# Inverting 64-row triangular blocks in pieces of 16, with gate copies and a weight split moved, in a one-layer RWKV-7 and window-attention step

## The chip, the cores and the metric

One core of one Trainium2 chip runs the whole program. The metric is device microseconds of one execution. The five engines have their own instruction queues, each worked off in order: PE (TensorE, matrix products; its weight loads are shown as PEld), DVE (VectorE), ACT (ScalarE), POOL (GpSimd) and SP (SyncE, which here only issues DMA transfers). A wait at the head of a queue holds everything behind it.

## The reference, cut to what matters

A prompt of 1024 tokens and 64 sample tokens (8 sequences of 8) pass through one layer: RMSNorm, one wide input projection, then two branches. Branch A is attention over a window of 128 with sinks. Branch B is RWKV-7: for each of 16 heads a 64x64 state is carried over the tokens.

```
z = ps + (prev - ps) * mu                      # token shift of r, k, v and two low-rank inputs
decay, a = f(w0 + tanh(wl) @ w2), sigmoid(a0 + al @ a2)      # the low-rank weights w2, a2
S_t = S_{t-1} * w_t + (S_{t-1} a_t) b_t^T + v_t k_t^T ;  y_t = S_t r_t
yb = (groupnorm(y) + bonus) * silu(gb)         # gb: the gate columns of the projection
out = x + (sigmoid(ma) * (ya @ w_out_a) + sigmoid(mb) * (yb @ w_out_b)) @ w_o ; y = RMSNorm(out)
```

The state is advanced by chunks of 64 tokens. Inside a chunk, the tokens depend on each other through a strictly triangular 64x64 matrix A made of the products of the keys, and the chunk needs the inverse of (I - A): one per chunk and head.

## The kernel before, in words

Products with the large weights are split: each fp32 operand is a high and a low part, and three products (hi·hi, hi·lo, lo·hi) are added (`mm3`, L183). A tile of 128 weight columns is `dense` (L190): three chunks of 364, 364 and 360 tokens, 24 matmuls each, into PSUM tiles `d` of which there are two; after each chunk a function `evac` empties the tile. The weights of the next tile are loaded ahead (`load_w`, L163): a DMA of `wraw`, ACT makes `whi`, POOL makes `wlo` (L171).

The program has four parts. `start` (L282) norms x and runs the first three tiles of weights; PE, SP and POOL take its instructions in the order in which they are written. At its end, for each of 8 groups, SP loads the low-rank weights (`lr`), ACT and DVE split them, and SP writes both parts to DRAM (`d_c`, L384 to L390). `rwkv` (L493) is branch B together with most of the input projection. `attention` (L1005) and `final` (L1314) follow.

`rwkv` works in 16 steps s = 4p + q: a pair p of head groups (2 groups x 2 heads) and a quarter q of the prompt (256 tokens, 4 chunks; in q = 3 also the 64 sample tokens). Each step has generators:

- `front` (L569): `quarter` twice (elementwise work on r, k, decay), `arrays`, `scores` (the products `A`, L775, of which the triangular parts are kept in `ab`), then the inversion, then `bonus` and `turn`.
- `invert` (L812): 32 diagonal blocks of 32x32 (16 matrices, two blocks each; 40 blocks in q = 3) go through DRAM (`s1`) into a layout of three partitions per block, and DVE substitutes row after row: 31 rounds of two instructions, L832 (product `Tt`) and L834 (sum `TR`), on up to 96 elements per partition. The inverses go back through DRAM (`s2`).
- `merge` (L839): loads them into `ti` (L855), transposes (DVE, L856), and makes the off-diagonal 32x32 quarter of each 64x64 inverse with two rounds of 16 small matmuls (`q_..a`, `q_..b`) and a DVE copy between (L867).
- `chain` (L877): four chunks in a row; in each PE and DVE hand to each other three times: `c<-vsu,X`, DVE copy `xs` (L910), `c<-xs,ti`, DVE copy `vsu` (L915), `c<-vsu,kbt`, DVE update `vsu` (L926).
- `posts` and `samples`: group norm and output of a step; the sample tokens.

Beside them runs `stream`: the dense tiles of the projection. Its evacuations are `shift_tile` (L398: two scaled copies by ACT, sum by POOL, and one column carried from the last chunk by DVE, L411), `gate` (L438: ACT makes the sigmoid in three passes from PSUM, then DVE multiplies it with the PSUM tile, L444, and SP writes `d_g`) and `spill` (L449: the same for gates of branch A at L460). Tiles `zz` and `pad` of these evacuations have two buffers each.

Two things set the order. PE's is written out by `drive` (L142): it keeps a clock of its own, adds a price for each matmul (`mm`, L111) and takes next the generator whose due time comes first; a generator says how long it has to wait (`yield mark, time`). So `merge` is placed `WI` = 38 after the mark `f` of its front, and its first matmul `WM` = 5 later; dense matmuls fill the time between. The order on DVE, ACT, POOL and SP comes from a scheduler by priorities: chains and merges 400000, fronts, samples and posts 200000, dense 0; `INV` is 0 here, so the inversion stands where its front stands.

Of the kernel before, what the change touches and what calls it, by code (L numbers as in the profile page):

```python
# [25 lines left out]
NG = 8  # L26
# [3 lines left out]
FRONT, CHAIN, SAMP, POST, DENSE, INV = 200000, 400000, 200000, 200000, 0, 0  # L30
# [10 lines left out]
WI, WD, WB, WA, WM, WH, WS, WP, WT, WR, WE = 38.0, 3.5, 4.0, 2.0, 5.0, 1.4, 2.4, 5.0, 10.0, 3.0, 12.0  # L41
# [40 lines left out]
class Prog:  # L82
# [199 lines left out]
    def start(self, xp, w0):  # L282
# [115 lines left out]
    def shift_tile(self, idx, ti, out):  # L398
# [5 lines left out]
        def evac(c0, c1, ps):  # L404
# [44 lines left out]
    def spill(self, idx, dst, kind="copy", scale=1.0):  # L449
# [3 lines left out]
        def evac(c0, c1, ps):  # L453
# [3 lines left out]
            else:  # L457
                self.sig_neg(t, t, ps, -1.0, 0.0)
                if kind == "silu":
                    nc.vector.tensor_tensor(t, ps, t, ALU.mult)  # L460
# [32 lines left out]
    def rwkv(self):  # L493
# [28 lines left out]
        for t in (self.ti, self.tss):  # L522
            nc.gpsimd.memset(t, 0.0)
        for t in self.xs:
# [44 lines left out]
    def front(self, s):  # L569
# [22 lines left out]
        s1 = self.dp.tile([2, 2 * nh, 32, 32], F32, name=f"s1{nm}")  # L592
        for h in range(2):
            for i in range(2):
                r = 64 * h + 32 * i
                nc.sync.dma_start(s1[i, h * nh:h * nh + nh].rearrange("n j t -> j n t"), f["ab"][r:r + 32, :nh, 32 * i:32 * i + 32])
        f["s1"], n2 = s1, 2 * nh
        with self.tc.high_priority(offset=INV):
            self.invert(nm, n2, f)
# [35 lines left out]
    def prefetch(self, g, q):  # L635
# [7 lines left out]
        nc.sync.dma_start(w2.bitcast(F32).rearrange("p x j c -> p x (j c)"), self.d_c[:, g])  # L643
# [168 lines left out]
    def invert(self, nm, n2, f):  # L812
# [3 lines left out]
        ab, s1 = f["ab"], f["s1"]  # L816
        nb = 2 * n2
        s2 = self.dp.tile([nb, 33, 32], F32, name=f"s2{nm}")
        np_ = 3 * nb
        M = [ep.tile([P, 16, 32 - 16 * x], F32, tag=f"TM{x}", name=f"TM{x}{nm}", bufs=1) for x in range(2)]  # L820
        R = ep.tile([P, 11, 32], F32, tag="TR", name=f"TR{nm}", bufs=1)
        tmp = ep.tile([P, 128], F32, tag="Tt", name=f"Tt{nm}", bufs=1)
        for x in range(2):
            for k in range(3):
                nc.sync.dma_start(M[x][:np_].rearrange("(b k) j t -> k b j t", k=3)[k],
                                  s1.rearrange("i n j t -> (i n) j t")[:, 16 * x:16 * x + 16, 16 * x:])
        nc.sync.dma_start(R[:np_], self.I["ri"][:np_].rearrange("p (a b) -> p a b", a=11))
        for s in range(31):
            w = 31 - s
            cc = s // 3 + 1  # L830
            tv = tmp[:np_, :cc * w].rearrange("p (c t) -> p c t", c=cc)
            nc.vector.tensor_tensor(tv, M[s // 16][:np_, s % 16:s % 16 + 1, s + 1 - 16 * (s // 16):].to_broadcast([np_, cc, w]),  # L832
                                    R[:np_, 0:cc, s:s + 1].to_broadcast([np_, cc, w]), ALU.mult)
            nc.vector.tensor_tensor(R[:np_, 0:cc, s + 1:32], R[:np_, 0:cc, s + 1:32], tv, ALU.add)  # L834
        for k in range(3):
            nc.sync.dma_start(s2.rearrange("b (c k) t -> k b c t", k=3)[k], R[:np_].rearrange("(b k) c t -> k b c t", k=3)[k])
        f["s2"] = s2

    def merge(self, s):  # L839
        nc = self.nc  # L840
        nm = f"{s // 4}_{s % 4}"
        yield f"f{s}", WI
        if s:
# [3 lines left out]
        f = self.fr[s]  # L847
        ab, nh = f["ab"], f["nh"]
        sv = f["s2"][:, :32, :].rearrange("(i n) j t -> i j n t", i=2)
        tv = self.ti.rearrange("p i c x -> p (i c) x")  # L850
        for h in range(2):
            r = 64 * h
            for i in range(2):
                b = r + 32 * i
                nc.sync.dma_start(tv[b:b + 32, :, b:b + 32], sv[i][:, h * nh:h * nh + 8, :])  # L855
            nc.vector.transpose(ab[r:r + 32, 0:8, 0:32], tv[r:r + 32, :, r:r + 32])  # L856
            if nh == 10:
                for i in range(2):
# [697 lines left out]
```

## Time and profile before

| | us |
|---|---|
| median of 3 runs | 1932.51 (1928.37 to 1935.75) |
| the profiled execution | 1925.88 |
| its span, first to last instruction | 1924.1 |
| PE busy / DVE / ACT / POOL in the span | 1665.7 / 1239.1 / 911.9 / 510.8 |
| mean granted clock of PE, of full speed | 0.929 |

A matmul's row gives its own duration, and matmuls overlap; distances between starts tell the rate. "Idle before" is the time in which the engine did nothing before an instruction, and the name behind "<-" is what ended the wait. The granted clock is 1.0 at 2.4 GHz and 0.5 at 1.2 GHz; means lie between.

### The profile page before, as it was taken

Reading aid. Unit: us, or ns where it says so; the run is one execution under the profiler, and the core shown is the slowest. Engines: PE = TensorE matmul, PEld = TensorE weight load, DVE = VectorE, ACT = ScalarE, POOL = GpSimd, SP = SyncE. Lnnn points to the kernel's source line nnn. Section 1 sums busy time; section 2 is a strip of 40 time slices with the busy share of each in tenths; the row PEclk is TensorE's granted clock in tenths of the full one; section 3 lists DMA queues with packets and bytes.
Section 4 is the critical chain, followed back from the end, with each engine's and each line's share of the span. In section 5 each row is a group of like instructions: output and inputs, shape, how many; then the busy total and the mean of one; then the engine's idle time right before and its main releaser. Section 6 shows DMA issues by size and latency. Waiting matters only on the chain.

```text
span 1924.1 us, 33459 instructions
## 1 busy us (share of the span) xinstructions
PE 1665.7 (87%) x11744; PEld 1570.1 (82%) x11744; DVE 1239.1 (64%) x3667; ACT 911.9 (47%) x2270; POOL 510.8 (27%) x654
## 2 busy tenths in 40 slices
PE   6839978868878878886987888799999999999997
PEld 4739977768777878876877888799999999899997
DVE  6202468768768877867778777874266777644543
ACT  5314544435445545544545556553466665522232
POOL 4236424323424432442343323233300010000000
PEclk7869989878989988987988999899999999999999
DMA  4233433324333433333333344223622343374531
GB/s 164 89 121 115 122 96 96 104 74 112 99 97 114 113 104 100 110 82 96 111 99 103 106 116 117 83 79 99 198 79 72 92 148 118 114 243 141 174 108 58
DMA packets 236795, 214.98 MB, mean 112 GB/s; under 512 B 134996, under 2 KB 205252, under 8 KB 236596
## 3 DMA queue, kind: packets, MB, share of 16 engines
q1 hardware_dynamic: 221844, 162.70, 29.4%
q0 software_dynamic: 14784, 50.15, 7.9%
q8 instruction: 93, 1.52, 0.3%
q14 instruction: 74, 0.61, 0.1%
HBM read 147.58 MB, written 67.16 MB: 112 GB/s over the span
## 4 chain that ended last, share of the span: by engine, by line
PE 48%; DVE 27%; DMA 8%; issue 7%; ACT 4%; POOL 3%; SPq 2%; DVEq 0%; POOLq 0%; ACTq 0%
PE d L110 29%; DVE Tt L832 6%; DVE TR L834 5%; PE wo L110 5%; PE c L110 2%; DVE vsu L926 2%; PE s L110 2%; DVE KB L711 2%; PE A L110 2%; PE o L110 2%; DMA wraw<-in_w 2%; PE pt L108 1%; DMA TM<-s 1%; PE y L110 1%; DMA lr<-in_lora 1%
## 5 line engine op out<-in xcount | busy, mean ns | idle before, releaser
L110 PE MATMUL d<-hhi,whi 128*128 128x364 f32 (+1 forms) x1656 | 588.9, 356 | 127.1 <-DVE gz L444 46.8
L110 PE MATMUL d<-hlo,whi 128*128 128x364 f32 (+1 forms) x1656 | 569.6, 344 | 10.2 <-DVE hlo L352 8.7
L110 PEld LDWEIGHTS d<-hhi,whi 128*128 128x128 f32 x1656 | 331.5, 200 | 138.4 <-DVE gz L444 50.1
L110 PEld LDWEIGHTS d<-hlo,whi 128*128 128x128 f32 x1656 | 331.2, 200 | 18.3 <-DVE hlo L352 13.2
L110 PE MATMUL d<-hhi,wlo 128*128 128x364 f32 (+1 forms) x1656 | 339.4, 343 | 0.0
L110 PEld LDWEIGHTS d<-hhi,wlo 128*128 128x128 f32 x1656 | 287.5, 197 | 3.9 <-issue 2.9
L171 POOL TENSOR_TENSOR wlo<-wraw,whi 128x1024 fp32r<-128x1024 f32 x56 | 137.1, 2448 | 201.9 <-ACT whi L170 74.1
L832 DVE TENSOR_TENSOR Tt<-TM,TR 96x90 f32<-96x90 f32 (+26 forms) x496 | 157.1, 317 | 23.1 <-DMA TM<-s 10.2
L834 DVE TENSOR_TENSOR TR<-TR,Tt 96x90 f32<-96x90 f32 (+26 forms) x496 | 135.6, 273 | 12.7
L170 ACT ACTIVATE whi<-wraw 128x1024 fp32r<-128x1024 f32 x90 | 95.0, 1056 | 85.3 <-PE d L110 61.3
L902 POOL TENSOR_TENSOR sp<-vsu,pc 64x128 f32<-64x128 f32 x128 | 63.2, 494 | 236.8 <-DVE vsu L926 218.6
L414 POOL TENSOR_TENSOR zz<-zz,pad 128x364 f32<-128x364 f32 (+1 forms) x75 | 71.6, 955 | 105.2 <-ACT zz L413 70.0
L1390 POOL TENSOR_TENSOR xr<-xr,frs 128x256 f32<-128x256 f32 x2 | 1.8, 932 | 342.6 <-ACT frs L1387 342.6
L926 DVE SCALAR_TENSOR_TENSOR vsu<-c,pc,sp 64x64 f32<-64x64 f32 x240 | 67.9, 283 | 26.7 <-PE c L110 23.3
L412 ACT ACTIVATE pad<-d,prm 128x364 f32<-128x364 f32 (+1 forms) x75 | 40.8, 543 | 91.4 <-PE d L110 58.1
L1129 ACT ACTIVATE sc<-sc,st 128x256 f32<-128x256 f32 (+1 forms) x128 | 61.8, 485 | 28.4 <-DVE st L1125 28.2
L110 PE MATMUL d<-yhi,whi 128*128 128x364 f32 (+1 forms) x192 | 63.8, 333 | 0.0
L110 PE MATMUL d<-ylo,whi 128*128 128x364 f32 (+1 forms) x192 | 63.8, 332 | 0.0
L110 PE MATMUL d<-ol,whi 128*128 128x364 f32 (+1 forms) x192 | 63.1, 329 | 0.7 <-DVE ol L230 0.7
L110 PE MATMUL d<-oh,whi 128*128 128x364 f32 (+1 forms) x192 | 63.2, 329 | 0.0
L711 DVE TENSOR_TENSOR KB<-e,sg 64x256 f32<-64x256 f32 x128 | 61.8, 497 | 1.2
L110 PEld LDWEIGHTS c<-vsu,kbt 128*128 128x128 f32 x256 | 37.7, 202 | 30.0 <-DVE vsu L915 29.3
(329 smaller groups left out, 3617.9 us busy)
## 6 DMA issues: line engine op xcount, KB each, us to landing
wraw<-in_w POOLq DMA_DIRECT2D x56, 512.0 KB, 4.1
wraw<-in_w SPq DMA_DIRECT2D x37, 512.0 KB
d_z<-zz POOLq DMA_DIRECT2D x48, 182.0 KB, 2.2
w<-d_c SPq DMA_DIRECT2D x32, 256.0 KB
zv<-d_z SPq DMA_DIRECT2D x48, 128.0 KB
d_m<-sp SPq DMA_DIRECT2D x32, 182.0 KB
stageo<-d_o SPq DMA_DIRECT2D x8, 544.0 KB
d_z<-zz POOLq DMA_DIRECT2D x24, 180.0 KB, 4.1
```

Of the source, the lines that this page charges most:

```text
L108: self.nc.tensor.transpose(out, lhsT, rhs)
L110: self.nc.tensor.matmul(out, lhsT=lhsT, rhs=rhs, **kw)
L170: nc.scalar.activation(hi, raw, AF.Copy)
L171: (nc.vector if self.dve_lo else nc.gpsimd).tensor_tensor(lo, raw, hi.bitcast(F32), ALU.subtract)
L412: nc.scalar.activation(pad[:, 1:1 + m], ps[:, :m], AF.Copy, scale=mu)
L414: nc.gpsimd.tensor_tensor(z[:, :m], z[:, :m], pad[:, 0:m], ALU.add)
L711: nc.vector.tensor_tensor(KB[hr, :4, j, :], self.v64(t)[hr], self.d64(Pi, 1)[hr], ALU.mult)
L832: nc.vector.tensor_tensor(tv, M[s // 16][:np_, s % 16:s % 16 + 1, s + 1 - 16 * (s // 16):].to_broadcast([np_, cc, w]), R[:np_, 0:cc, s:s + ...
L834: nc.vector.tensor_tensor(R[:np_, 0:cc, s + 1:32], R[:np_, 0:cc, s + 1:32], tv, ALU.add)
L902: nc.gpsimd.tensor_tensor(sp[h], vsu[h, c, :, h], pc[h, c].unsqueeze(2).to_broadcast([64, 2, HD]), ALU.mult)
L926: nc.vector.scalar_tensor_tensor(dst, pn[h, i, h], pc[h, c, i:i + 1], sp[h, i], ALU.mult, ALU.add)
L1129: nc.scalar.activation(sc[k], sc[k], AF.Exp, bias=st[:, 0, k:k + 1], accum_out=st[:, 1, k:k + 1])
```

## The change: what it does

The diff has four parts. (1) The inversion substitutes in diagonal blocks of 16: two partitions per block, 15 rounds of two DVE instructions on at most 36 elements. In q = 3 the sample matrices are inverted by a second call. `merge` now puts the inverses into `dinv` with 8 loads (4 from SP, 4 from POOL), and builds 32x32 and then 64x64 inverses by four rounds of small matmuls (32, 32, 16 and 16) with DVE work between; only its last part waits for the chain of the step before. (2) The gates of branch B, and of branch A in `spill`, are copied from PSUM by ACT, and POOL multiplies; POOL writes `d_g`. (3) The low-rank weights are no longer split in `start`: in a group's first quarter `prefetch` loads the raw weights into a `zz` buffer, splits them on ACT and DVE into the tile that is used, and writes them to `d_c` for the other three quarters. (4) The column carried between chunks is copied by ACT. Beside that: `INV` is 150000, `WI` is 24, and the planner's price of a 32-row matmul is 0.024.

```diff
-FRONT, CHAIN, SAMP, POST, DENSE, INV = 200000, 400000, 200000, 200000, 0, 0
+FRONT, CHAIN, SAMP, POST, DENSE, INV = 200000, 400000, 200000, 200000, 0, 150000
...
-        self.clk += max(n / 2190, 0.085) if rhs.dtype == F32R else ...
+        self.clk += 0.024 if rhs.shape[0] == 32 else max(n / 2190, 0.085) if rhs.dtype == F32R else ...
...  start
-        for g in range(NG):
-            raw, hi, lo = (xp.tile([P, 364], F32, tag="sq", name=f"l{x}{g}", bufs=4)[:, :2 * P] for x in "rhl")
-            nc.sync.dma_start(raw, self.I["lora"][:, g].rearrange("p j c -> p (j c)"))
-            nc.scalar.activation(hi.bitcast(F32R), raw, AF.Copy)
-            nc.vector.tensor_tensor(lo.bitcast(F32R), raw, hi, ALU.subtract)
-            for x, t in enumerate((hi, lo)):
-                nc.sync.dma_start(self.d_c[:, g, x], t)
...  shift_tile
-                nc.vector.tensor_copy(pad[:, 0:1], prev[0][:, 364:365])
+                nc.scalar.activation(pad[:, 0:1], prev[0][:, 364:365], AF.Copy)
...  gate (spill: the same with `sx`, without the DMA)
-            self.sig_neg(t, t, ps, -1.0, 0.0)
-            nc.vector.tensor_tensor(t, ps, t, ALU.mult)
-            nc.sync.dma_start(self.d_g[g][:, c0:c1], t)
+            x = ep.tile([P, 369], F32, tag="pad", name=f"gx{g}_{c0}", bufs=2)[:, :c1 - c0]
+            nc.scalar.activation(x, ps, AF.Copy)
+            self.sig_neg(t, t, x, -1.0, 0.0)
+            nc.gpsimd.tensor_tensor(t, x, t, ALU.mult)
+            nc.gpsimd.dma_start(self.d_g[g][:, c0:c1], t)
...  prefetch
-        nc.sync.dma_start(w2.bitcast(F32).rearrange("p x j c -> p x (j c)"), self.d_c[:, g])
+        w2v = w2.bitcast(F32).rearrange("p x j c -> p x (j c)")
+        if q:
+            nc.sync.dma_start(w2v, self.d_c[:, g])
+        else:
+            raw = ep.tile([P, 364], F32, tag="zz", name=f"w2r{nm}", bufs=2)[:, :2 * P]
+            nc.sync.dma_start(raw, self.I["lora"][:, g].rearrange("p j c -> p (j c)"))
+            nc.scalar.activation(w2[:, 0].rearrange("p j c -> p (j c)"), raw, AF.Copy)
+            nc.vector.tensor_tensor(w2[:, 1].rearrange("p j c -> p (j c)"), raw, w2v[:, 0], ALU.subtract)
+            nc.sync.dma_start(self.d_c[:, g], w2v)
...  invert
+        for a in range(2):
+            for k in range(2):
+                nc.sync.dma_start(M[nb * a:nb * a + nb].rearrange("(b k) j t -> k b j t", k=2)[k], s1[:, 16 * a:16 * a + 16, 16 * a:16 * a + 16])
-        for s in range(31):
-            w = 31 - s
-            cc = s // 3 + 1
+        for s in range(15):
+            w = 15 - s
+            cc = s // 2 + 1
...  merge
+        for n0, s2 in zip((0, 8), f["s2"]):
+            nn = 2 if n0 else 8
+            for a in range(2):
+                for g in range(4):
+                    o = 32 * g + 16 * a
+                    (nc.gpsimd if a else nc.sync).dma_start(D[o:o + 16, n0:n0 + nn, 16 * a:16 * a + 16], s2[a, g].rearrange("n j t -> j n t"))
+        nc.vector.transpose(flat(dt), flat(D))
+        yield None, 0.0, "t"
+        ... 32 matmuls (ab x dt), DVE e = product x moff
+        yield None, WH, "t"
+        ... 32 matmuls (e x D), DVE T = product + D, DVE transpose of T
+        yield None, WH + 1.0, "t"
+        ... 16 matmuls (ab x dt), DVE copies
+        if s:
+            yield f"c{s - 1}", 0.0
+        if s > 1:
+            yield f"p{s - 2}", 0.0
+        ... POOL copies T into ti (and D into tss in q = 3)
+        yield None, WH, "t"
+        ... 16 matmuls, ACT copies into ti
```

## Rows read from the trace of the kernel before

**Rows 1.** Windows: engine busy us (instructions), PE's granted clock, DMA share, GB/s.

```profile
130.00:1342.00 1212.00, 1028.46 (x7587) 972.01 (x7586) 869.40 (x2675) 592.89 (x1509) 441.41 (x563) 0.92 0.36 102
1342.00:1392.00 50.00, 49.77 (x296) 48.52 (x296) 15.77 (x27) 21.61 (x44) 16.92 (x18) 1.00 0.58 180
1392.00:1924.00 532.00, 518.11 (x3562) 492.45 (x3560) 307.70 (x879) 247.16 (x613) 8.23 (x8) 0.99 0.39 124
```

**Rows 2.** Waits of PE from 130 to 1392: us in total, times, longest.

```profile
PE d L110 <- DVE gz L444: 45.6, 6, 16.5
...
PE c L110 <- DVE xs L910: 24.6, 17, 3.2
PE d L110 <- ACT sho L423: 20.3, 7, 10.4
PE c L110 <- DVE vsu L915: 20.3, 21, 3.3
PE d L110 <- ACT sp L220: 9.1, 2, 6.0
```

**Rows 3.** Timelines of SP, POOL and PE, end of the start: start us, us.

```profile
78.88 0.38 SPq L386 DMA_DIRECT2D lr<-in_lora  x1
...
117.92 0.14 POOL L754 MEMSET ams<- 64x64 f32 x1 [36.25 <-DMA d_c<-ll]
...
123.84 0.57 POOL L169 DMA_DIRECT2D wraw<-in_w  x1
...
129.51 0.67 PE L110 MATMUL d<-hhi,whi 128*128 128x364 f32 x1 [38.81 <-ACT whi L170]
```

**Rows 4.** Timelines of ACT, DVE and PE around one gate chunk.

```profile
380.87 0.51 ACT L222 ACTIVATE gz<-gz 128x364 f32<-128x364 f32 x1
...
401.43 0.53 DVE L444 TENSOR_TENSOR gz<-d,gz 128x364 f32<-128x364 f32 x1
...
402.01 0.67 PE L110 MATMUL d<-hhi,whi 128*128 128x364 f32 x1 [16.53 <-DVE gz L444]
402.48 0.51 PE L110 MATMUL d<-hlo,whi 128*128 128x364 f32 x1
402.78 0.51 PE L110 MATMUL d<-hhi,whi 128*128 128x364 f32 x1
```

**Rows 5.** Timeline of ACT, one shift-tile chunk.

```profile
685.54 0.51 ACT L412 ACTIVATE pad<-d,prm 128x296 f32<-128x296 f32 x1 [8.59 <-DVE pad L411]
```

**Rows 6.** Groups by line, whole span: count, busy us, mean ns, idle before.

```profile
L832 DVE TENSOR_TENSOR Tt<-TM,TR 96x90 f32<-96x90 f32 (+26 forms) x496 | 157.1, 317 | 23.1 <-DMA TM<-s 10.2
L834 DVE TENSOR_TENSOR TR<-TR,Tt 96x90 f32<-96x90 f32 (+26 forms) x496 | 135.6, 273 | 12.7
...
L787 DVE TENSOR_TENSOR am<-A,rco 128x256 f32<-128x256 f32 x64 | 27.1, 423 | 38.0 <-ACT ab L782 37.3
L414 POOL TENSOR_TENSOR zz<-zz,pad 128x364 f32<-128x364 f32 (+1 forms) x75 | 71.6, 955 | 105.2 <-ACT zz L413 70.0
```

**Rows 7.** Timelines of PE and DVE, step 8 from scores to merge.

```profile
775.33 1.13 PE L110 MATMUL A<-X,KB 64*128 64x128 f32 x14 [0.32 <-ACT sp L221]
...
787.98 0.19 DVE L832 TENSOR_TENSOR Tt<-TM,TR 96x30 f32<-96x30 f32 x1
...
822.28 0.16 DVE L834 TENSOR_TENSOR TR<-TR,Tt 96x11 f32<-96x11 f32 x1
...
832.30 0.43 DVE L856 STREAM_TRANSPOSE ab<-ti 32x256 f32<-32x256 f32 x1 [1.67 <-issue]
...
838.19 0.69 PE L110 MATMUL q_0b<-ti,ab 32*32 32x32 f32 x32
```

**Rows 8.** Timelines of POOL and DVE, the same moment.

```profile
600.73 2.60 POOL L171 TENSOR_TENSOR wlo<-wraw,whi 128x1024 fp32r<-128x1024 f32 x1
...
601.00 2.41 DVE L832 TENSOR_TENSOR Tt<-TM,TR 96x64 f32<-96x64 f32 x1
```

**Rows 9.** The chain of waits in order of time: one stretch in the final part.

```profile
1722.03 93.61 PE d L110 x561
```

More of the change, by code (lines that the diff above doesn't have):

```diff
@@ L457, in evac @@
             else:
-                self.sig_neg(t, t, ps, -1.0, 0.0)
+                x = ps
                 if kind == "silu":
-                    nc.vector.tensor_tensor(t, ps, t, ALU.mult)
+                    x = ep.tile([P, 369], F32, tag="pad", name=f"sx{idx}_{c0}", bufs=2)[:, :c1 - c0]
+                    nc.scalar.activation(x, ps, AF.Copy)
+                self.sig_neg(t, t, x, -1.0, 0.0)
+                if kind == "silu":
+                    nc.gpsimd.tensor_tensor(t, x, t, ALU.mult)
             for d, a, b in dst:
@@ L521, in rwkv @@
         self.xs = [cp.tile([P, 4, 4, HD], F32, name=f"X{x}") for x in range(4)]
-        for t in (self.ti, self.tss):
+        self.dinv = cp.tile([P, 10, 32], F32, name="dinv")
+        self.moff = cp.tile([P, 32], F32, name="moff")
+        for t in (self.ti, self.tss, self.dinv):
             nc.gpsimd.memset(t, 0.0)
+        nc.sync.dma_start(self.moff, self.I["moff"])
         for t in self.xs:
@@ L591, in front @@
             yield from self.scores(2 * p + i, q, i, f)
[L592 to L597, printed above, removed]
+        f["s2"] = []
         with self.tc.high_priority(offset=INV):
-            self.invert(nm, n2, f)
+            for n0, nn in ((0, 8), (8, 2))[:1 + q // 3]:
+                f["s2"].append(self.invert(f"{nm}{n0}", f["ab"], n0, nn))
         self.mark(f"f{s}")
@@ L837, in invert @@
-        f["s2"] = s2
+            nc.vector.tensor_tensor(R[:np_, 0:cc, s + 1:16], R[:np_, 0:cc, s + 1:16], tv, ALU.add)
+        for k in range(2):
+            nc.sync.dma_start(s2.rearrange("a g n (c k) t -> k (a g n) c t", k=2)[k], R[:np_].rearrange("(b k) c t -> k b c t", k=2)[k])
+        return s2
     def merge(self, s):
-        nc = self.nc
+        nc, ep = self.nc, self.ep
         nm = f"{s // 4}_{s % 4}"
         yield f"f{s}", WI
+        f = self.fr[s]
+        ab, nh = f["ab"], f["nh"]
@@ new lines, in merge, with flat @@
+        groups = [slice(32 * g, 32 * g + 32) for g in range(4)]
+        D, dt = self.dinv, ep.tile([P, 8, 32], F32, tag="dt", name=f"dt{nm}", bufs=1)
+        for n0, s2 in zip((0, 8), f["s2"]):
+            nn = 2 if n0 else 8
+            for a in range(2):
+                for g in range(4):
+                    o = 32 * g + 16 * a
+                    (nc.gpsimd if a else nc.sync).dma_start(D[o:o + 16, n0:n0 + nn, 16 * a:16 * a + 16], s2[a, g].rearrange("n j t -> j n t"))
+        def flat(t):
+            return t[:, 0:8].rearrange("p n t -> p (n t)")
@@ new lines, in merge @@
+        nc.vector.transpose(flat(dt), flat(D))
+        yield None, 0.0, "t"
+        pq = self.ps("t", f"q{nm}a").rearrange("p (n x) -> p n x", x=32)
+        for n in range(8):
+            for g, r in enumerate(groups):
+                i = 32 * (g % 2)
+                self.mm(pq[r, n, :], lhsT=ab[r, n, i:i + 32], rhs=dt[r, n, :], start=True, stop=True)
+        e = ep.tile([P, 8, 32], F32, tag="dt", name=f"e{nm}", bufs=1)
+        nc.vector.tensor_tensor(e, pq[:, 0:8], self.moff.unsqueeze(1).to_broadcast([P, 8, 32]), ALU.mult)
@@ new lines, in merge @@
+        yield None, WH, "t"
+        pq = self.ps("t", f"q{nm}b").rearrange("p (n x) -> p n x", x=32)
+        for n in range(8):
+            for g, r in enumerate(groups):
+                self.mm(pq[r, n, :], lhsT=e[r, n, :], rhs=D[r, n, :], start=True, stop=True)
+        T = ep.tile([P, 8, 32], F32, tag="tc", name=f"tc{nm}", bufs=1)
+        nc.vector.tensor_tensor(T, pq[:, 0:8], D[:, 0:8], ALU.add)
+        dt = ep.tile([P, 8, 32], F32, tag="dt", name=f"du{nm}", bufs=1)
+        nc.vector.transpose(flat(dt), flat(T))
@@ L843, in merge @@
+        yield None, WH + 1.0, "t"
+        pq = self.ps("t", f"q{nm}c").rearrange("p (n x) -> p n x", x=32)
+        for n in range(8):
+            for r in (0, 64):
+                self.mm(pq[r + 32:r + 64, n, :], lhsT=ab[r:r + 32, n, 32:64], rhs=dt[r:r + 32, n, :], start=True, stop=True)
+        for r in (0, 64):
+            nc.vector.tensor_copy(dt[r + 32:r + 64], pq[r + 32:r + 64, 0:8])
         if s:
@@ L1423, in _consts @@
     c[:, C_SCAN:C_SCAN + 332] = s
-    ri = np.zeros((P, 11, 32), np.float32)
-    for q in range(P):
-        for a in range(11):
-            if 3 * a + q % 3 < 32:
-                ri[q, a, 3 * a + q % 3] = 1.0
+    ri = np.zeros((P, 8, 16), np.float32)
+    for a in range(8):
+        ri[p, a, 2 * a + p % 2] = 1.0
+    moff = ((p[:, None] % 32 >= 16) & (np.arange(32)[None, :] < 16)).astype(np.float32)
     c[:, C_EPS] = 1e-6
@@ L1432, in _consts @@
     bc = np.stack([same, np.eye(P) - same / 64.0], 1).astype(np.float32)
-    return c, ri.reshape(P, 352), bc
+    return c, ri.reshape(P, 128), bc, moff
 def prep(inp):
```

61 lines of the change are left out of this document (19 added, 42 removed).

## The prediction, made before the changed kernel was run

> **What bounds the kernel now.** I read the windows first, cut at the stages [rows 1]. From 1392 on PE is busy 518 of 532 us at full clock; the change touches nothing there. From 1342 to 1392 it is 49.8 of 50: the dense tiles that were left over when the last chain had ended. The 1212 us from 130 to 1342 are another matter: PE is busy 1028.5 us, so it idles 183.5, and its mean clock of 0.92 means 16% of the time, some 194 us, at the lower level. DVE is at 869 us (72%). Because the order on PE leaves dense matmuls to the end, a step that gets shorter saves nothing by itself: it moves dense work from between the steps to the end. The time of this stage is PE's own work plus the waits that stand at the head of its queue, plus what it loses at the low clock after them. So I count the change in PE's waits and in PE's work.
>
> The waits of PE come next [rows 2]. The largest is for the gate's multiply on DVE (45.6 us in 6 waits), then two of the chain's hand-overs to DVE (24.6 and 20.3), then an evacuation by ACT (20.3 in 7). A wait of 38.8 us stands in the timelines of the start [rows 3]: the low-rank weights are split in eight laps of SP, from 78.88 on, about 4.9 us each up to 117.92, (117.92 - 78.88) / 8. POOL waits 36.25 us for the last write, clears buffers for 5.9 us, and only then issues the load of the next weights at 123.84; PE starts at 129.51.
>
> **The change part by part.** *Start.* Without the laps POOL is free when its wait began, at 117.92 - 36.25 = 81.7. It clears its buffers in 5.9 us and the new one in some 0.4 (an estimate from the 0.14 us of a 64x64 clear in [rows 3] and its larger size); from the load's issue to PE it was 129.51 - 123.84 = 5.7. That gives 93.7 in place of 129.5, where PE had run dry at 129.51 - 38.81 = 90.7. I take -35.8. At most the whole wait goes (-38.8); at least -30, if other work of the start comes late.
>
> *Gate.* In [rows 4] ACT has finished the sigmoid at 381.4 (380.87 + 0.51), and the PSUM tile is released only when DVE comes to the multiply at 401.43: it stands behind 20 us of front work and substitution in DVE's queue. With ACT's copy the tile is free before the sigmoid starts. The 45.6 us go. After such a wait PE runs at the low clock: matmuls 402.78 - 402.48 = 0.30 us apart, against 93.61 / 561 = 0.167 in a busy stretch [rows 9]; 4 us of that lose 1.8 us, for five long waits about 10. ACT's own queue takes some back: two waits for a `spill` sigmoid on ACT cost 9.1 [rows 2]; I take +8. Sum -47, between -56 and -20.
>
> *Carried column.* ACT stood 8.59 us in front of a `pad` copy for DVE [rows 5]. Of the 20.3 us of waits for shift-tile evacuations I take 12 off; two small DVE operations stay in two of three chunks, so between 0 and -20.
>
> *Inversion on DVE.* Before: (157.1 + 135.6) / 16 = 18.3 us per step [rows 6], in 62 instructions. After: 30 of at most 36 elements. Undisturbed, 30 elements take 0.19 us and 11 take 0.16 [rows 7]; the means in [rows 6] are about 1.25 times the undisturbed rows, so 30 x 0.18 x 1.25 = 6.8 us. The four steps with samples have 60 instructions, about 12 us. Saved: 12 x 11.5 + 4 x 6.3 = 163 us; new are two operations on a 128x256 PSUM tile per step at 0.42 (L787 in [rows 6]), 14 us, and gates and columns take off another 20. DVE falls from 869 to about 700 us, 72% to 58%. What that is worth is what its queue costs PE: 24.6 + 20.3 = 45 us in the chain [rows 2]. If such a wait goes as the ratio of busy to idle share (72/28 = 2.6 before, 58/42 = 1.4 after), it falls by 46%, 21 us; the low clock after 38 such waits gives some 11 more. I take -32, between 0 and -70 (all of them, with clock and the merges' own waits).
>
> *More work on PE.* Per step 96 small matmuls in place of 32. Sixteen of them (32 records, each fp32 matmul has two) take 0.69 us in [rows 7], 43 ns each. 64 x 43 ns x 16 steps = 44 us is the upper end. The first two rounds use four partition groups instead of two; if that halves the price it is 22 us. I take +26. Below nothing it can't go, since instructions are added and none goes.
>
> *Three more hand-overs per merge* (e, T with its transpose, and the copy that was there before now behind them): 48 in all. The chain's 64 `xs` hand-overs cost 24.6 / 64 = 0.38 us each, the `vsu` ones 0.32 [rows 2]. At the old price 17, with the freer DVE +12; all of them late by 1 us would be +45; 0 if the planner's gaps (1.4 and 2.4) cover all. Behind each on PE stands everything, dense matmuls and the chain alike.
>
> *When the merge comes.* Before, from the end of the scores (775.33 + 1.13 = 776.5) to the transpose was 832.30 - 776.5 = 55.8 us for a planned 38 + 5 [rows 7], a ratio of 1.3. After: scores to first substitution was 11 us, now 9.8 with four loads in place of six; 30 instructions, mixed with the chain's, 9 to 11; write, loads and transpose 9.9 before, about 10 now. That is 29 to 31 for a planned 24, ratio 1.25. So I expect no more waiting here: 0, from -14 to +60.
>
> *POOL.* 33 multiplies of 0.955 (L414 in [rows 6]), 64 copies of a tile quarter at some 0.35 (estimated from the same row by size), and 24 + 80 DMA issues of 0.57 [rows 3]: 113 us on top of 441 in 1262, 35% to 44%. In its queue stand the `wlo` that the next dense tile needs, the sums of the shift tiles and the chain's `sp`. I take +5, up to +25.
>
> In [rows 8] a DVE operation of 0.2 us takes 2.41 while POOL runs `wlo` for 2.60. The Trainium skill, SBUF — State Buffer, "SBUF: two separate sides", says that POOL and a DVE instruction with two SBUF inputs share one port pair as an exclusive lock, and that the loser blocks for the whole instruction; the rows agree. It speaks against moving multiplies and copies to POOL: if the 54 us of new POOL arithmetic all blocked DVE, DVE's relief would be 115 instead of 169, and the sum below would be 10 us worse.
>
> *Split at first use.* Eight times an ACT and a DVE pass come behind the load, and a `zz` buffer of the evacuations is held meanwhile: +5, from 0 to +20.
>
> **Sum**, against the profiled execution of 1925.9: -35.8 - 47 - 12 - 32 + 26 + 12 + 5 + 5 = -79, so 1847. That execution lay 6.6 us (0.3%) below the median of 1932.5; for the median the forecast is 1847 + 6.6, rounded to 1850.
>
> **The rivals.** *DVE's queue was the bound of the stage.* For it: 72% busy, and nearly all waits in [rows 2] name it or ACT behind it. If two thirds of the 183 us of idle go, and half of a clock loss of some 45, while PE's work rises by 22: 1926 - 36 - 122 - 22 + 22 = 1768. Against it: every step still hands over 12 times in the chain. Chance 0.18.
>
> *The wait moves to the merge.* The plan gives it 24 us; if the loads come at 36, PE stands there 6 us longer in each of 16 steps, 96 us, part of which replaces waits for gates that are no longer there: 1847 + 45 = 1892. For it: ratio 1.3 already before. Chance 0.20.
>
> *Slower: POOL's loads block its queue.* Four of the eight loads in each merge are issued by POOL, which waits there for DVE's last substitution and the write. If the scheduler puts them ahead of a `wlo`, the next dense tile stands still as long. To turn -79 into +15 it takes 94 / 16 = 5.9 us of idle PE in each step; it decides from there: 1941. Against it: a tile is loaded ahead, and POOL is idle more than half of the time. Chance 0.06.
>
> *The waits come back elsewhere and nothing is left but the start*, against added PE work: 1926 - 36 + 26 + 12 = 1928. Chance 0.05.
>
> **How the numbers follow.** The forecast's own case, 1805 to 1885, has 0.51. The range 1780 to 1900 takes in it, the merge rival and the upper part of the DVE rival; about 0.2 lies outside. No change that a measurement tells is within 0.5%, 1923 to 1942. Faster: 0.51 + 0.18 + 0.20 + a part of the last = 0.90; within: 0.05; slower: 0.05.
>
> **What would show it.** In the changed trace PE's wait at the end of the start is about 3 us, not 38.8; no wait of PE names the gate's multiply; the substitution has 30 instructions per call and under 8 us busy; DVE is below 60% in the stage; a merge shows four rounds of small matmuls within some 10 us; dense matmuls run alone for longer than 50 us after the last chain. Wrong would be: the stretch before each merge's first round with waits of over 3 us in most steps; POOL waiting on the substitution with `wlo` behind it; or PE's idle time in the stage still above 150 us.

## The result and the profile after

The changed kernel took 1862.69 us (median of four executions, 1856.91 to 1870.40) against 1931.93 for the kernel before: a ratio of 0.9644, 95% interval 0.9601 to 0.9687, some 69 us faster. In a later set of runs (after_again, below) the ratio was 0.962. The forecast was 1850 us, between 1780 and 1900. The profiled execution has a span of 1857.9 us, 66.2 less than before.

The windows, cut at the same events as [rows 1] (start of the fifth dense tile, end of the last chain, end of the stage, end):

```profile
94.00:1264.00 1170.00, 1016.08 (x9523) 959.47 (x9521) 766.37 (x2255) 608.15 (x1577) 536.20 (x767) 0.94 0.36 101
1264.00:1335.00 71.00, 71.00 (x425) 69.75 (x424) 16.06 (x24) 35.95 (x67) 28.23 (x29) 1.00 0.53 163
1335.00:1858.00 523.00, 511.82 (x3545) 486.87 (x3543) 305.00 (x877) 243.38 (x610) 8.33 (x8) 0.99 0.39 124
```

The start is 130 - 94 = 36 us shorter. The stage has 1170 + 71 = 1241 us in place of 1262, so 21 less: PE idles 153.9 instead of 183.8 (minus 30) and is busy 1087.1 instead of 1078.2 (plus 9). The dense work alone at the end of the stage grew from 50 to 71 us, so half of the 42 us by which the chains end sooner within the stage is dense work that has only moved. The last part is 9 us shorter, though nothing in it was changed; in after_again it was 4 us longer than here, so I draw nothing from it.

PE's waits in the stage, the view of [rows 2]:

```profile
PE q_1a L110 <- DVE dt L863: 25.6, 4, 10.0
PE q_2a L110 <- DVE dt L863: 22.1, 4, 9.6
PE q_0a L110 <- DVE dt L863: 20.4, 4, 7.1
PE c L110 <- DVE xs L939: 20.1, 12, 5.6
PE lo L110 <- DVE sg L690: 15.9, 3, 6.4
PE c L110 <- DVE vsu L944: 9.7, 8, 2.7
...
PE q_3a L110 <- DVE dt L863: 5.4, 3, 2.6
...
PE q_3a L110 <- DVE Tt L839: 3.5, 1, 3.5
```

The gate's 45.6 us are gone, and so are all but 2 of the evacuation's 29.4 (`sho` and `sp` in [rows 2]). What has grown is the wait of the merges' first rounds, `q_0a` to `q_3a`: 25.6 + 22.1 + 20.4 + 5.4 + 3.5 = 77.0 us, where the kernel before had 6.1 + 4.6 + 3.7 = 14.4. The rounds behind it (`q_..b` to `q_..d`) wait about 3 us in all sixteen steps.

The end of the start, POOL and PE, to be read beside [rows 3]:

```profile
89.04 2.72 POOL L528 MEMSET X<- 64x256 f32 x8
91.74 2.38 POOL L171 TENSOR_TENSOR wlo<-wraw,whi 128x1024 fp32r<-128x1024 f32 x1
```

```profile
93.81 0.33 PE L110 MATMUL d<-hhi,whi 128*128 128x364 f32 x1
```

POOL clears its buffers without the wait of 36.25 us, and PE goes on at 93.81; the forecast had 93.7.

Step 9 from the end of the scores to the merge, DVE, SP and PE, to be read beside [rows 7] (start, duration, in brackets the idle time before and what ended it):

```profile
806.19 0.17 DVE L839 TENSOR_TENSOR Tt<-TM,TR 128x15 f32<-128x15 f32 x1
...
818.98 0.17 DVE L841 TENSOR_TENSOR TR<-TR,Tt 128x8 f32<-128x8 f32 x1
...
828.52 0.45 DVE L863 STREAM_TRANSPOSE dt<-dinv 128x256 f32<-128x256 f32 x1 [5.34 <-DMA dinv<-s]
```

```profile
793.36 1.82 SPq L827 DMA_DIRECT2D s<-ab  x4
...
823.07 1.74 SPq L860 DMA_DIRECT2D dinv<-s  x4
```

```profile
791.98 1.13 PE L110 MATMUL A<-X,KB 64*128 64x128 f32 x14 [1.46 <-DVE X L794]
...
829.02 1.07 PE L110 MATMUL q_1a<-dt,ab 32*32 32x32 f32 x64 [10.02 <-DVE dt L863]
834.03 1.06 PE L110 MATMUL q_1b<-dinv,e 32*32 32x32 f32 x64
837.87 0.69 PE L110 MATMUL q_1c<-du,ab 32*32 32x32 f32 x32
840.67 0.69 PE L110 MATMUL q_1d<-tc,du 32*32 32x32 f32 x32
```

The substitution takes 12.96 us from its first to its last instruction. From the end of the scores (791.98 + 1.13 = 793.11) to the first round it is 35.9 us: 13.1 pass on the way to DVE and 9.9 on the way back, with writes and loads issued by SP and POOL, their landing, and other issues of SP between them. Over the sixteen steps the distance is 24.9 to 35.9 us with a mean of 30; the forecast had 29 to 31.

### The profile page after: what moved, and what is told of

Same layout as the page of the kernel before. It is cut to its first block, busy times and chain, and to the rows that moved or that the text cites. A ratio compares the mean times of both kernels' runs of the same rounds, so it can differ in the third digit from the quotient of the medians.

```text
span 1857.9 us, 37541 instructions
## 1 busy us (share of the span) xinstructions
PE 1669.4 (90%) x13792; PEld 1574.9 (85%) x13792; DVE 1129.1 (61%) x3224; ACT 935.2 (50%) x2353; POOL 619.8 (33%) x872
## 4 chain that ended last, share of the span: by engine, by line
PE 55%; DVE 17%; DMA 5%; issue 3%; ACT 3%; POOL 1%; SPq 1%; DVEq 0%; POOLq 0%; ACTq 0%
PE d L110 32%; PE wo L110 5%; PE c L110 3%; DVE Tt L839 3%; DVE TR L841 2%; DVE KB L717 2%; DMA dinv<-s 2%; PE s L110 2%; PE y L110 2%; PE A L110 2%; PE o L110 2%; DMA s<-TR 1%; PE pt L108 1%; DVE vsu L955 1%; PE ss_d L110 1%
## 5 line engine op out<-in xcount | busy, mean ns | idle before, releaser
L110 PE MATMUL d<-hhi,whi 128*128 128x364 f32 (+1 forms) x1656 | 575.6, 348 | 6.0 <-ACT hhi L349 3.0
L110 PE MATMUL d<-hlo,whi 128*128 128x364 f32 (+1 forms) x1656 | 558.9, 338 | 12.5 <-DVE hlo L352 8.7
L110 PE MATMUL d<-hhi,wlo 128*128 128x364 f32 (+1 forms) x1656 | 344.6, 345 | 0.0
L110 PEld LDWEIGHTS d<-hlo,whi 128*128 128x128 f32 x1656 | 322.5, 195 | 20.0 <-DVE hlo L352 13.0
L110 PEld LDWEIGHTS d<-hhi,whi 128*128 128x128 f32 x1656 | 322.6, 195 | 10.9 <-ACT hhi L349 3.9
L931 POOL TENSOR_TENSOR sp<-vsu,pc 64x128 f32<-64x128 f32 x128 | 54.3, 424 | 137.5 <-DVE vsu L955 116.2
L839 DVE TENSOR_TENSOR Tt<-TM,TR 128x30 f32<-128x30 f32 (+3 forms) x300 | 79.5, 265 | 22.5 <-DMA TM<-s 12.5
L841 DVE TENSOR_TENSOR TR<-TR,Tt 128x30 f32<-128x30 f32 (+3 forms) x300 | 74.0, 247 | 9.5 <-DVE Tt L839 0.2
L171 DVE TENSOR_TENSOR wlo<-wraw,whi 128x1024 fp32r<-128x1024 f32 x34 | 41.5, 1221 | 55.4 <-DMA ys<-d_y 25.7
L860 POOL DMA_DIRECT2D dinv<-s x80 | 42.6, 540 | 68.2 <-DMA s<-TR 68.2
L1069 POOL TENSOR_TENSOR ylo<-ys,yhi 128x364 fp32r<-128x364 f32 (+1 forms) x6 | 6.5, 1085 | 174.1 <-ACT yhi L1068 174.1
```

The lines of the kernel that those rows point to most:

```text
L171: (nc.vector if self.dve_lo else nc.gpsimd).tensor_tensor(lo, raw, hi.bitcast(F32), ALU.subtract)
L839: nc.vector.tensor_tensor(tv, M[:np_, s:s + 1, s + 1:16].to_broadcast([np_, cc, w]), R[:np_, 0:cc, s:s + 1].to_broadcast([np_, cc, w]), AL ...
L841: nc.vector.tensor_tensor(R[:np_, 0:cc, s + 1:16], R[:np_, 0:cc, s + 1:16], tv, ALU.add)
L860: (nc.gpsimd if a else nc.sync).dma_start(D[o:o + 16, n0:n0 + nn, 16 * a:16 * a + 16], s2[a, g].rearrange("n j t -> j n t"))
L931: nc.gpsimd.tensor_tensor(sp[h], vsu[h, c, :, h], pc[h, c].unsqueeze(2).to_broadcast([64, 2, HD]), ALU.mult)
```

## The experiments

The three parts of the change (split, gates with the carried column, inversion with `INV`, `WI` and the planner's price) were run alone and in pairs. The edits are shown shortened, some lines in words. Ratios to the kernel before on the same chip, each with an interval of about plus or minus 0.0025 (0.0043 for the first run of all three):

| parts made | ratio | median, us |
|---|---|---|
| split | 0.9905 | 1913.1 |
| gates | 0.9816 | 1896.4 |
| inversion | 0.9747 | 1883.1 |
| split + gates | 0.9724 | 1877.4 |
| inversion + gates | 0.9718 | 1876.9 |
| inversion + split | 0.9621 | 1856.5 |
| all three | 0.9644, again 0.9620 | 1862.7, 1857.4 |

Alone, the parts take off 20.1, 36.8 and 50.1 us, together 107; all three take off 69 to 73.

### The split alone (only_split)

```diff
 start
-        for g in range(NG):  ... lr, split, write d_c
 prefetch
+        if q: load w2 from d_c   else: load raw, split on ACT and DVE, write d_c
```

> The kernel before with one part of the change alone: the eight low-rank weight splits leave the start and are made at the first use of each pair. Theory A (the parts add up; the start's 36.3 us wait for the memsets' queue is all that this part takes): first matmul of the fifth dense tile near 93.8 us instead of 129.5, the stage after it as long as before, 1893 to 1900 us (ratio 0.980 to 0.984). Theory B (the split at first use, with its DMA, activation and subtraction, delays the four first steps of a pair by 5 us or more each): 1910 to 1925 us, with waits of the low-rank matmuls (lo) grown by 15 to 25 us.

Measured: 1913.1 us, 0.9905 (0.988 to 0.993). The fifth dense tile starts at 95.4, as theory A says; the time is that of theory B, but not by waits of `lo`, which hardly grew. The largest piece of the loss sits at a gate. PE's waits from 1010 to 1032:

```profile
PE d L110 <- DVE gz L437: 16.0, 1, 16.0
```

ACT and DVE ahead of it:

```profile
1010.81 0.42 ACT L642 ACTIVATE w<-w2r 128x256 fp32r<-128x256 f32 x1 [4.38 <-DMA w2r<-in_lora]
```

```profile
1011.26 0.42 DVE L643 TENSOR_TENSOR w<-w2r,w 128x256 fp32r<-128x256 f32 x1 [2.98 <-ACT w L642]
...
1030.00 0.53 DVE L437 TENSOR_TENSOR gz<-d,gz 128x364 f32<-128x364 f32 x1
```

Before, the wait at this gate was 3.6 us, so this one place costs 12.4 us. Here ACT stands for the raw weights and DVE for ACT, and the gate's multiply stands behind some 19 us of other work of DVE (1011.26 to 1030.00). The gate's last sigmoid pass on ACT comes late too: it begins at 1024.50, 8 us after the pass before it has ended. Of the 34 us won at the start 20 are left; the rest of the loss is spread over the stage, and I have not traced it.

### The gates alone (only_gates)

```diff
-            nc.vector.tensor_copy(pad[:, 0:1], ...)          # carried column
+            nc.scalar.activation(pad[:, 0:1], ..., AF.Copy)
-            self.sig_neg(t, t, ps, -1.0, 0.0); nc.vector.tensor_tensor(t, ps, t, ALU.mult); nc.sync.dma_start(d_g, t)
+            x = copy of ps by ACT; self.sig_neg(t, t, x, -1.0, 0.0); nc.gpsimd.tensor_tensor(t, x, t, ALU.mult); nc.gpsimd.dma_start(d_g, t)
```

> The kernel before with the second part alone: gates and SiLU tiles copied out of PSUM by ScalarE and multiplied on GpSimd, the carried column copied by ScalarE; the old inversion and the old start stay. Theory A (the gate waits of 45.6 us, and some of the evacuations' waits, are the part's own): waits on gz gone, 1875 to 1888 us (-45 to -57). Theory B (the matmuls that no longer wait arrive earlier at the merge, whose inversion still takes 33 us, so most of it comes back as wait there): gz waits gone but the waits of the merge's first round (q_0b to q_3b group) and of the chain grown by 25 us or more, 1905 to 1925 us.

Measured: 1896.4 us, 0.9816 (0.9791 to 0.9841), between the two. The gate waits are gone; PE waits 4.0 us for ACT's new copies. The merge's first rounds wait 24.6 us (16.8 + 4.2 + 3.6) where they waited 14.4, and the chain's two hand-overs 52.1 where they waited 44.9: a growth of 17 us, short of theory B's 25. The evacuations still wait:

```profile
PE c L110 <- DVE vsu L921: 28.4, 25, 3.4
PE c L110 <- DVE xs L916: 23.7, 17, 3.2
...
PE d L110 <- ACT sp L220: 12.6, 3, 6.0
PE d L110 <- ACT sho L423: 9.4, 6, 3.2
```

With `zz` (36.8 in the stage, less the 27.6 at its start) that is 12.6 + 9.4 + 9.2 = 31.2 us; before it was 9.1 + 20.3 + 8.7 = 38.1. The 20.3 that my term for the carried column named (`sho`) fell by 10.9; `sp` grew by 3.5.

### The inversion alone (only_inv)

Its edit is the diff's `invert` and `merge` with the three numbers, and neither gates nor start.

> The kernel before with the third part alone: substitution in blocks of 16, three more merge rounds on TensorE, the planned latency cut from 38 to 24; the old gates and the old start stay. Theory A (it takes about 32 us of DVE hand-overs off the chain and pays about 27 us of added matmuls and some merge waits): 1915 to 1935 us, neither clearly faster nor slower. Theory B (DVE's queue behind the 62 long substitution instructions was the bound, so this part carries most of the stage's gain): 1890 to 1905 us, gate waits fall from 45 to under 25 us without the gates being touched. Theory C (the plan of 24 is short, the merge is waited for each step): 1940 us or more, with 60 us or more of waits before the merge's first round.

Measured: 1883.1 us, 0.9747 (0.9724 to 0.9771): a larger gain than any of the three theories. Theory B's sign came (gate waits under 25 us), and so did theory C's (60 us or more before the merges), though not its time. PE's waits in its stage:

```profile
PE q_1a L110 <- DVE dt L856: 25.3, 4, 9.0
PE q_2a L110 <- DVE dt L856: 21.1, 4, 9.1
PE q_0a L110 <- DVE dt L856: 20.7, 4, 6.5
PE c L110 <- DVE vsu L937: 12.0, 9, 2.7
...
PE d L110 <- DVE gz L444: 10.7, 3, 8.1
PE c L110 <- DVE xs L932: 9.9, 12, 1.8
...
PE d L110 <- ACT sho L423: 2.8, 3, 1.4
```

The gates and the evacuations were not touched, and yet their waits fell, from 45.6 to 10.7 and from 38.1 to about 3; the chain's two fell from 44.9 to 21.9. The merges' first rounds went the other way: with `q_3a` they wait 73.5 us in place of 14.4. Up to the end of the last chain PE idles 142 us here, in place of 183.5.

That the waits fell because the substitution no longer stood in DVE's queue is only in part what the rows show. During the 45.6 us of gate waits in the kernel before, DVE was busy for 44.4, but for 8.8 of them with the substitution; during the 38.2 us of evacuation waits it spent 2.7 on it, and during the chain's 44.9 us some 20. The rest was mostly the front's elementwise work, such as `KB` and `X`. And a part of the gates' waiting has moved to the merge. At the gate of [rows 4], where PE stood 16.53 us, it now stands twice:

```profile
368.58 1.08 PE L110 MATMUL q_2a<-dt,ab 32*32 32x32 f32 x64 [9.08 <-DVE dt L856]
...
384.01 0.67 PE L110 MATMUL d<-hhi,whi 128*128 128x360 f32 x1 [8.12 <-DVE gz L444]
```

The sigmoid was done at 365.70 and the multiply came at 383.42, 17.7 us later, where it was 20.0 before. At the gate that had waited 14.8 us PE now stands 9.0 us before a merge and not at all at the gate. So the chain's gain agrees with a shorter substitution. For the gates and evacuations there are two readings, which no run separates: DVE is through earlier, or PE comes later because it stands at the merge first. The new plan (`WI`, the price), which moves the merges in PE's order, was not run without the new inversion either.

### The gates taken out of the changed kernel (inv_split)

> The changed kernel with its gate part undone (gates and SiLU multiplied on VectorE out of PSUM again, the carried column copied by VectorE); new inversion and new start stay. Alone, the three parts gave 20, 37 and 50 us, together 70: they overlap. Theory A (the gate waits came only from VectorE's queue standing behind the substitution, which the shorter substitution cures by itself; only_inv had 10.7 us of them left): 1845 to 1865 us, the same as the changed kernel (1862) or a little faster, gate waits under 15 us. Theory B (the gate part still carries its 37 us beside the others): 1885 to 1900 us.

Measured: 1856.5 us, 0.9621 (0.9597 to 0.9644); the changed kernel 0.9644 and 0.9620. Theory A. The gate part, worth 37 us alone and as much beside the split (0.9905 to 0.9724, 35 us), is worth nothing measurable beside the new inversion. The stage's window says why, inv_split first, then the changed kernel:

```profile
94.00:1330.00 1236.00, 1088.18 (x9944) 1029.64 (x9945) 786.16 (x2352) 627.22 (x1568) 524.79 (x742) 0.94 0.37 105
```

```profile
94.00:1335.00 1241.00, 1087.08 (x9945) 1029.22 (x9944) 782.43 (x2278) 644.11 (x1644) 564.43 (x795) 0.94 0.37 104
```

PE has the same work and idles 148 us against 154. POOL took on 40 us (524.79 to 564.43) and ACT 17, and DVE was relieved of 74 instructions but of 3.7 us only (786.16 to 782.43), though in inv_split's stage the gates' multiplies (21) take 11.1 us, those of `spill` (9) 4.8 and the column copies (46) 6.9, together 22.8. A part came back on other lines of DVE, inv_split first:

```profile
L711 DVE TENSOR_TENSOR KB<-e,sg 64x256 f32<-64x256 f32 x128 | 64.0, 518 | 1.1
L740 DVE TENSOR_TENSOR X<-zr,Pp 64x256 f32<-64x256 f32 x64 | 31.4, 490 | 1.1 <-ACT Pp L694 0.4
```

```profile
L717 DVE TENSOR_TENSOR KB<-e,sg 64x256 f32<-64x256 f32 x128 | 68.0, 549 | 1.1
L746 DVE TENSOR_TENSOR X<-zr,Pp 64x256 f32<-64x256 f32 x64 | 38.3, 599 | 1.0 <-ACT Pp L700 0.4
```

Those two lines alone are 4.0 + 6.9 = 10.9 us longer. A second pair of runs goes the same way by less: 508 to 523 ns and 483 to 549 ns from r_first to after_again, 6 us. In the changed kernel 64 of these 192 operations overlap with arithmetic of POOL and last 864 ns in the mean; the other 128 last 416. The changed kernel shows a case like [rows 8] in step 9, DVE and POOL at one moment:

```profile
814.66 2.39 DVE L839 TENSOR_TENSOR Tt<-TM,TR 128x24 f32<-128x24 f32 x1
```

```profile
814.62 2.40 POOL L171 TENSOR_TENSOR wlo<-wraw,whi 128x1024 fp32r<-128x1024 f32 x1 [1.15 <-ACT vsu L816]
```

24 elements that take about 0.19 us elsewhere in the same step take as long as POOL's 1024. That a DVE operation with two inputs in SBUF and POOL shut each other out for a whole instruction is what the Trainium skill says (SBUF — State Buffer, "SBUF: two separate sides"); these rows agree with it, and nothing in the sums above rests on it.

### The old inversion with new gates and new start (gates_split)

> The changed kernel with its inversion part undone (substitution over 31 steps, one merge round on VectorE less, plan 38, priority as before); new gates and new start stay. Theory A (gates moved off VectorE no longer stand behind the substitution, so the old one costs little; the start's 36 us come in full since no gate is hit by the shift as in only_split, where one gate wait grew from 3.6 to 16 us): 1855 to 1868 us, as the changed kernel. Theory B (the shorter substitution has a gain of its own through the chain's hand-overs): 1875 to 1890 us.

Measured: 1877.4 us, 0.9724 (0.9702 to 0.9745), theory B. Here the split and the gates simply add (20.1 + 36.8 = 56.9 against 54.1). The inversion is worth another 15 to 20 us beside them: the waits that it takes away there are no longer the gates' but the chain's and the evacuations'.

### A longer plan for the merge (wi30)

```diff
-WI, ... = 24.0, ...
+WI, ... = 30.0, ...
```

> The changed kernel with one number of the planner altered: the latency planned from scores to merge is 30 instead of 24 (30 us is the mean that the changed kernel's trace shows). Theory A (the 74 us that TensorE waits before the first merge round are a plan too short): these waits fall from 74 to under 30 us and the time by 20 to 40 us, to 1823 to 1843 us. Theory B (little independent dense work is left to put there, or a later merge delays the chain by as much as is gained): the waits fall but others (xs, vsu, sho) grow by as much, 1855 to 1868 us. Theory C (the later merge lengthens the stage by 16 steps of 6 us less what is hidden): over 1870 us.

Measured: 1862.8 us, 0.9637 (0.9609 to 0.9666), theory B. The merge waits are gone from the head of the list, and others stand there:

```profile
PE c L110 <- DVE xs L939: 23.0, 16, 4.7
PE lo L110 <- DMA w<-d_c: 20.1, 7, 5.8
PE A L110 <- DVE X L794: 15.7, 15, 2.2
```

In the changed kernel `A` waited 5.3 us and `lo` 21 in all; here `lo` waits 40, and the merges' first rounds 6. With the merge planned later, PE comes too early to the front work of the next step instead: the sum of waits and work in the stage stays (1241.8 us against 1241.2).

### The wait for the inverses taken away (nowait)

```diff
 invert
-        for k in range(2): nc.sync.dma_start(s2 ...[k], R ...[k])
 merge
-        dma_start(D[...], s2[a, g].rearrange("n j t -> j n t"))
+        dma_start(D[...], self.I["con"][0:16, C_ID:C_ID + 16].unsqueeze(1).to_broadcast([16, nn, 16]))
```

> The changed kernel with the wait for the inverses taken away: they are not written back, and the blocks that the merge needs are loaded from a constant (the identity), by as many loads on the same queues, so the substitution still runs but nothing waits for it. Theory A (the 74 us that TensorE waits before the first merge rounds are the loss of the changed kernel): those waits under 15 us and the time down by 45 to 75 us, 1790 to 1818 us. Theory B (the order leaves the same work and the waits move to the chain's own hand-overs, xs, vsu and the low-rank matmuls, as when the plan was set to 30): 1838 to 1865 us, merge waits gone and others grown by 40 us or more.

Measured: 1828.6 us, 0.9477 (0.9453 to 0.95), between the theories. Against the changed kernel's 0.9644 and 0.9620 that is 28 to 32 us. The merges' first rounds have left the list; at its head stand now:

```profile
PE c L110 <- DVE xs L937: 20.8, 13, 3.4
PE ss_d L110 <- DVE ve L996: 15.1, 4, 7.3
```

PE's idle time fell from 153.9 to 122.1 us in the stage, and not by 77. So the merge waits are worth at most some 30 us here: the other part, when it goes, is waited elsewhere.

### The priority of the substitution (inv0)

`INV` from 150000 back to 0 in the changed kernel.

> The changed kernel with the substitution's raised priority (150000) set back to 0; nothing else. Theory A (the priority keeps other work of VectorE out of the substitution, 11.4 us from its first to its last instruction for 7.9 us of work): the substitution stretches to 15 us or more, the merge is waited for by 5 us more a step, 1880 to 1910 us. Theory B (with few and short instructions in between it hardly matters): 1855 to 1872 us.

Measured: 1864.1 us, 0.9653 (0.9632 to 0.9674), theory B. The first substitution of a step lasts as long as with the priority (11.2 us in the mean, 11.4 with it).

### Shorter ways to the merge (r_first, two_queues)

Both start from inv_split.

```diff
 r_first: the load of R stands ahead of the writes of s1
 two_queues: that, and
-            nc.sync.dma_start(s1[...])   nc.sync.dma_start(M[...])   nc.sync.dma_start(s2[...])
+            (nc.gpsimd if g % 2 else nc.sync)...   (nc.gpsimd if a else nc.sync)...   (nc.gpsimd if k else nc.sync)...
```

> The changed kernel without its gate part, as in inv_split (1856.5 us, ratio 0.962), and with the load of the substitution's start values moved ahead of the writes of its inputs; the later loads on SP then go one earlier. Theory A (SP's row of loads is a part of the 30 us from scores to merge: about 0.7 to 1.2 us a step come out of it, and nowait gave 34 us for some 20 us a step): 1848 to 1856 us (ratio 0.957 to 0.961). Theory B (what is saved is spent in other waits): no change, 1854 to 1860 us.

Measured: 1856.9 us, 0.9614 (0.9592 to 0.9635): theory B, no change.

> As r_first, and half of the loads and stores around the substitution (two of four writes of its inputs, two of four loads, one of two stores) issued on GpSimd instead of SP. Theory A (the row of loads on one queue costs 2 to 3 us a step): 1842 to 1852 us (ratio 0.954 to 0.959), merge waits (the rounds' first matmuls on dt) down from 66 to 40 us. Theory B (GpSimd stands before loads that wait for the scores and the substitution, and the low-order weight halves and sums behind them come late): 1862 to 1890 us, with waits of dense matmuls on wlo, zz or sp of 10 us or more.

Measured: 1880.7 us, 0.9730 (0.9707 to 0.9754), 24 us slower than r_first: theory B's time. The merge waits did go, further than theory A had it, from 73 us in r_first to 6.7 + 3.3 + 3.0 = 13. PE's waits and POOL's:

```profile
PE c L110 <- DVE xs L933: 33.1, 19, 3.5
PE d L110 <- DVE gz L437: 29.2, 4, 10.8
```

```profile
POOL s L837 <- DVE TR L835: 22.9, 7, 5.7
POOL s L837 <- DVE pad L404: 18.9, 4, 5.7
```

POOL stands 42 us before its new stores of the inverses, and another 15.6 and 14.5 before the writes and loads of the inputs: 72 us. Its wait before the loads of the inverses fell from 67.4 us in r_first to 19.1, so before all issues of the inversion it stands 91 us in place of 67. What came late on PE is not `wlo`, `zz` or `sp`, as theory B had it, but the chain's `xs` (9.0 in r_first) and the gates (10.1). By which steps POOL's standing reaches those two I have not traced. The second reading in only_inv fits here too: the substitution is the short one, the standing before the merges is gone, and the gates and `xs` are waited for again.

### All but the start (inv_gates) and the changed kernel again (after_again)

> The changed kernel with its start undone: the eight low-rank weights are split before the stage again. only_split gave 20 us for a start 34 us shorter, because the gates met the substitution in other places (one wait grew from 3.6 to 16.0 us). Theory A (with gates and substitution changed there is no such wait to run into, so the start is worth its full 31 to 37 us here): 1893 to 1900 us (ratio 0.979 to 0.983), and slower than only_inv (1883), the gate part being worth nothing beside the inversion. Theory B (the split at first use costs the stage some 15 us wherever it is made): 1877 to 1886 us.

Measured: 1876.9 us, 0.9718 (0.9694 to 0.9741), at the lower edge of theory B's time. The split is worth 1876.9 - 1857.4 = 19.5 us here. Part of the difference from 36 is that the gates on ACT and POOL shorten the start by themselves: its fifth dense tile starts at 122.1, not 129.5, so only 28 us are left for the split. In the profiled executions the two stages are equally long (1234.8 and 1234.5), so theory B's loss in the stage isn't seen there; the medians leave some 8 us that I can't place.

> The changed kernel once more, beside the three others on one chip, so that they can be compared with it and not only with the kernel before. Theory A (the gate part is worth nothing beside the new inversion): ratio 0.961 to 0.966, within 0.3% of inv_split's 0.962. Theory B (it still helps): below 0.959.

Measured: 1857.4 us, 0.9620 (0.9597 to 0.9642), theory A: beside inv_split and r_first (0.9621, 0.9614) there is nothing to choose. Apart from nowait, which leaves a dependence out, no version beats the changed kernel by more than can be measured; inv_split equals it with less work on POOL and ACT.

## Why the prediction was right, and where its terms were not

The sum of -79 us was near the measured -69 and -73, but that is in part luck: two of its terms hung on the wrong part, and their errors cancelled.

- **Start, -35.8.** In the trace -35.7, to the step: PE dry or busy until 93.81 instead of 93.7. What reaches the end is less: 20 us alone, 24 beside the inversion (0.9747 to 0.9621), 18 to 20 beside the gates, where only 28 were to be had. Of the loss only the gate wait in only_split is shown, 12.4 us.
- **Gate, -47, carried column, -12, POOL, +5.** Together -54. The gate's waits did go, all of them; ACT took back 4.0 + 3.5 us in only_gates, where +8 was reckoned; `sho` fell by 10.9, near the column's 12. But the part alone gave -37, and beside the inversion -6 (0.9747 to 0.9718) or nothing (inv_split). The terms missed 17 us more of waits at the merge and the chain, and the 10 us that they gave to the low clock did not come (below).
- **Inversion on DVE, -32; this is the mis-sized term.** I wrote that "what that is worth is what its queue costs PE" and then counted only the chain's 45 us. The gate's 45.6 and, by ACT's waits for DVE, the evacuations' 38.1 stood behind DVE as well, and they fell with this part too, whether cured or moved to the merge. Alone, with PE's added work paid, the part gave -50 where my terms for it (-32 + 26 + 12 + 0) say +6. The chain's own waits fell by 23 in only_inv, as forecast (21), and by 15 in the changed kernel. The 11 us that the term gave to the low clock after these waits rest on no row.
- **More work on PE, +26.** The merges' matmuls were busy 25.2 us before and 52.0 after: +26.8.
- **Three more hand-overs, +12.** About 3 us of waits: the planner's gaps cover them. The four rounds take 11 to 14 us.
- **When the merge comes, 0.** The latency was as forecast, the wait was not: 77.0 us where the rows before had 14.4. It is not the new gates that bring PE to the place early: only_inv, with the old ones, has 73.5. This is the rival "the wait moves to the merge", put too high in price: nowait gives back 28 to 32 us, and wi30 none.
- **Split at first use, +5.** PE waits 3.0 + 1.7 us for the split weights (`w`).
- **The low clock.** The dense matmuls show it, the first group of the page after, whose count and work are those of before:

```profile
L110 PE MATMUL d<-hhi,whi 128*128 128x364 f32 (+1 forms) x1656 | 575.6, 348 | 6.0 <-ACT hhi L349 3.0
```

  Before, the same 1656 took 588.9 us, 356 ns each, and the mean granted clock of the span was 0.929 against 0.951 now. With the second group (569.6 to 558.9) that is 24 us less of busy time, with the third (339.4 to 344.6) 19, which pays for most of the merges' added 26.8. Of the dense work of the stage 99.5 us ran at 1.2 GHz before, 66.3 in the changed kernel. This goes with the inversion and not with the gates: in only_inv the group takes 578.1 us, in gates_split 586.8, and in only_gates, where the gate's waits are gone,

```profile
L110 PE MATMUL d<-hhi,whi 128*128 128x364 f32 (+1 forms) x1656 | 588.7, 356 | 67.5 <-ACT zz L413 38.5
```

  So the gate's term was wrong to reckon with 10 us of clock. Why the dense work meets the low clock less beside the new inversion stays open.

Of the signs that I named, the start, the gate, the 30 instructions ((79.5 + 74.0) / 20 calls = 7.7 us busy) and the dense work after the last chain (71 us) came as said. The four rounds took 11 to 14 us, not some 10. DVE stayed at 766.37 / 1170 = 65.5%, not below 60%: its busy time fell by 103 us where 169 were reckoned (the substitution's by 139, from 292.7 to 153.5, where 163 were), and the stage is shorter. And the sign for "wrong" came too: 11 of 16 merges are waited for by more than 3 us, and PE's idle time in the stage is 153.9, not below 150. The DVE rival was wrong about the size, as only 30 of the 184 us of idle time went, and the rows bear its cause out for the chain, not for the gates and the evacuations.

## What to carry to other kernels

When several waits end on one engine, don't count each as its own: one edit took the waits of gates, evacuations and chain down together, and the edit made for the gates was then worth nothing beside it. Read what the engine does during those waits before naming the cause: the substitution filled 9 of 46 us at the gates and 20 of 45 in the chain. Look, too, at where the waiting engine stands instead: here 59 us of the waits came back before the merges. Parts that cure the same wait must be tried alone and in pairs, since their gains overlap (107 us for 69 to 73). And a wait in the list need not be worth its length: 77 us before the merges were worth 28 to 32, and nothing at all where only their place in PE's order was moved.

## What the runs showed of the hardware

Gate and `spill` multiplies and column copies of 22.8 us, taken off DVE with the multiplies going to POOL, took 3.7 us off DVE's busy time, and other operations of DVE grew longer (518 to 549 ns and 490 to 599 ns for the same tiles; 864 ns where they overlap with POOL's arithmetic, 416 where not). And half of the inversion's transfers issued by POOL instead of SP cost 24 us, with POOL standing 91 us before such issues in place of 67; that the loss came by this standing is not shown.
